# A planner that runs the chain between two stages first and holds long weight splits back for it

## The chip, the cores and the metric

The kernel runs on one core of one Trainium2 chip. The metric is the device time of one execution in microseconds (us), given as the median of the runs. PE is TensorE (matmuls), DVE is VectorE, ACT is ScalarE, POOL is GpSimd, SP is the engine that issues the transfers.

## The reference, cut to what matters

Two blocks of two layers each work on the same 256 tokens of width 1024, all in float32. Every layer is a mixer followed by a gated feed-forward network, and between any two of them stands the same small step: the product is scaled by a gate, added to the residual x, normed per token, and scaled and shifted per channel, which gives the input h of the next stage.

```python
h = modulate(rmsnorm(x, g_mix_pre[i]), sh_a, sc_a)
qkv = jnp.einsum('bsd,de->bse', h, w_qkv[i])
...
o = jnp.einsum('bse,ed->bsd', merge_heads(o), w_o[i])
x = x + gt_a[:, None, :] * rmsnorm(o, g_mix_post[i])
h = modulate(rmsnorm(x, g_ffn_pre[i]), sh_f, sc_f)
gate = jnp.einsum('bsd,df->bsf', h, w_ffn_gate[i])
up = jnp.einsum('bsd,df->bsf', h, w_ffn_up[i])
gate = causal_depthwise_conv(gate, w_conv[i], b_conv[i])
y = jnp.einsum('bsf,fd->bsd', jax.nn.silu(gate) * up, w_ffn_down[i])
x = x + gt_f[:, None, :] * rmsnorm(y, g_ffn_post[i])
```

The second block has the same frame without the norm behind the product, with a differential attention over tokens and context in its first layer and a short convolution in its second. In order there are eight stages: attention, feed-forward, attention, feed-forward, differential attention, feed-forward, short convolution, feed-forward.

## The kernel before, in words

**Arithmetic.** Each float32 operand of a large product is split into a high and a low part (`split`: a cast on ACT gives the high part, a subtraction on DVE the low part), and a product is three matmuls: high by high, high by low, low by high. A weight arrives from HBM as a chunk of 128 x 2048 (tile `w`, 1 MB). Each half of it is one long split: `wh` on ACT (128x1024) and `wl` on DVE (128x1024). The per-channel scales are made beside this by long DVE instructions over weight chunks (`w<-w,rows,vec`, 128x1024, called dots here). The small splits have names of their own: `oh`, `ol` and `doh`, `dol` for attention outputs, `yh`, `yl` for the feed-forward, `zhl` for the convolution, `h0h`, `h0l`, `h1h`, `h1l` for h.

**The boundary.** At the end of a stage, `last_products` adds the last terms to the accumulators `acc`: both halves of token tile 0 first, then token tile 1. `tail` then does, for token tile 0 and then 1: on DVE `u<-acc,rows` (gate) and `x` (residual) for two halves of 512; on ACT a sum of squares (`junk<-x`); on POOL a power (`ssr`); on DVE `u<-x,ssr` (the normed x); on PE eight transposes (`tps<-eye,u`); then on DVE and ACT scale and shift (`hf`) and the split into `h0h` and the rest. Where the product is normed too (the first block), a first sum of squares (`junk<-acc`) and power stand ahead of `x`. The next stage begins with `first_tiles`: two weight tiles over token tile 0 and then over token tile 1 (`fp`, 96 matmuls of 128x256), which are transposed afterwards (`fpt`). `rowps` are transposes that spread a gate over all rows. The two boundaries ahead of the second attention and of the differential attention have no `fp`; PE has other products there.

The boundaries with `fp` are named here A (first attention to feed-forward), C (second attention to feed-forward), E (differential attention to feed-forward), F (feed-forward to short convolution) and G (short convolution to feed-forward); B and D are the two without.

**The order.** The program is first recorded (`Rec.record`), each operation with a number `i` in program order and a modelled cost. `Rec.schedule` then plans all engines at once: at each model time, an engine that is free takes, of the operations whose inputs have arrived, the one with the lowest number (the heap `ready`); operations whose last input is already under way stand in `pending` with the time at which they arrive. Tiles come from a few lists of fixed size (`SLOTS`; PSUM has four banks of class `mm`, and a pair of score tiles `dz` takes two of them at once); weight splits (group `W`) and chunks (class `K8`) are handed out strictly in program order. `emit` writes the instructions in the planned order, so each engine works through a fixed queue on the chip. All profile rows carry the one line 573 of `emit`; a group is told by its tiles. In the model a cast `wh` costs 946 ns, a subtraction `wl` 1135 ns and the power 464 ns; a result of DVE reaches DVE's next instruction after another 127 ns.

Of the kernel before, what the change touches and what calls it, by code (L numbers as in the profile page):

```python
# [21 lines left out]
KT = D // P  # L22
# [237 lines left out]
class Op:  # L260
    __slots__ = ("i", "eng", "fn", "args", "kw", "deps", "outs", "tiles", "cost", "waits", "start", "end", "act", "dma")


class Rec:
# [4 lines left out]
    def __init__(self):  # L269
        self.ops, self.limit, self.count, self.after = [], 0, 0, None  # L270
        self.follow = {}
# [31 lines left out]
    def record(self, eng, fn, args, kw):  # L303
        op = Op()
        op.i, op.eng, op.fn, op.args, op.kw = len(self.ops), self.ENGINES[eng], fn, args, kw
        op.outs, op.deps, op.tiles, op.dma, op.act = [], {}, [], 0, 0
        outs = [kw[k] for k in ("out", "accum_out") if isinstance(kw.get(k), VAP)]
        ins = [v for k, v in kw.items() if k not in ("out", "accum_out") and isinstance(v, VAP)]
        pos = [a for a in args if isinstance(a, VAP)]
        if pos and "out" not in kw:  # L310
            outs.append(pos[0])
            pos = pos[1:]
        ins += pos
        if fn == "matmul" and not kw["start"]:
            v = outs[0]
            if any(w[0] & v.mask and w[1] < v.parts[1] and w[2] > v.parts[0] for w in v.t.writes):
                ins.append(v)
        for v in ins:
            self.access(op, v, False)
        for v in outs:  # L320
            self.access(op, v, True)
        if fn == "matmul" and kw["start"]:
            v = outs[0]
            for w in v.t.writes:
                if w[3] is not op and w[1] < v.parts[1] and w[2] > v.parts[0]:
                    op.deps.setdefault(w[3], 1)
        if self.after is not None:
            op.deps.setdefault(self.after, 1)
        for t in op.tiles:
            t.ops.append(op)  # L330
        op.cost = self.cost(op, outs, ins, args, kw)
        self.ops.append(op)
# [71 lines left out]
    def schedule(self, slots):  # L404
# [59 lines left out]
        while left:  # L464
# [14 lines left out]
            for e in engines:  # L479
                while pending[e] and pending[e][0][0] <= now:  # L480
# [3 lines left out]
                    else:  # L484
                        heapq.heappush(ready[e], (i, op))
            for e in engines:
# [6 lines left out]
                while ready[e]:  # L493
                    op = heapq.heappop(ready[e])[1]
                    if op in taken:
                        continue
                    lack = fits(op)
# [114 lines left out]
class Builder:  # L612
# [334 lines left out]
    def tail(self, acc, which, post, nxt):  # L947
        nc = self.nc
        g = self.gates[which]
        self.h = self.new_ht("h")  # L950
        for t in range(2):
# [4 lines left out]
            for a, b, c in zip(self.halves(u), y, self.halves(g)):  # L956
                nc.vector.tensor_tensor(out=a, in0=b, in1=c, op=ALU.mult)
            for a, b in zip(self.halves(u), self.halves(self.x[t])):
# [4 lines left out]
            self.put_ht(self.h, self.normed(self.x[t], u, self.xe[t]), t, *nxt)  # L963
        self.finish(*MODS)
# [201 lines left out]
    def attention1(self, i):  # L1166
# [13 lines left out]
        for it in range(KT + 2):  # L1180
# [17 lines left out]
            if 0 <= j < KT:  # L1198
# [3 lines left out]
                with nc.together():  # L1202
# [4 lines left out]
                    for hh in range(2):  # L1207
                        nc.tensor.matmul(
                            op[sl[hh], 128:256], lhsT=vs[1][:, cs[hh]], rhs=ats[hh][:, 256:384], start=False, stop=True
                        )  # L1210
                os_[j] = self.split(op[:, 0:256], S, "o")
            if it % 2 == 1 and it < KT:
# [15 lines left out]
    def ffn(self, b, i, nxt):  # L1228
# [5 lines left out]
        for f in range(NF + 1):  # L1234
# [14 lines left out]
            if f < NF:  # L1249
                s = self.sb.tile([P, S], F32, tag="s", name="s")  # L1250
# [13 lines left out]
                ys[f] = self.split(y, S, "y")  # L1264
                if f % 2 == 0:
# [116 lines left out]
    def diff_attention(self):  # L1382
# [67 lines left out]
        for it in range(U + VLAG + 3):  # L1450
# [3 lines left out]
            if it < U:  # L1454
# [23 lines left out]
                if m == 1:  # L1478
                    for hh in range(2):
# [8 lines left out]
                        es[it - 1 + hh] = p[0]  # L1488
            u = it - VLAG
# [21 lines left out]
            if 0 <= u < U and u % 4 >= 2:  # L1511
# [7 lines left out]
                if j % 2 == 0:  # L1519
                    w2[j], w2[j + 1] = wo.take()  # L1520
            j = it - WOFROM
# [22 lines left out]
    def short_conv(self):  # L1544
# [4 lines left out]
        for f in range(KT + 1):  # L1549
# [23 lines left out]
            if f % 2 == 1:  # L1573
# [4 lines left out]
                for k in range(2):  # L1578
                    z = self.sb.tile([P, S], F32, tag="z", name="z")
                    nc.vector.tensor_tensor(out=z, in0=zz[f - 1 + k], in1=ps[:, k * S : (k + 1) * S], op=ALU.mult)  # L1580
                    hl = self.sb.tile([P, 2 * S], F32R, name="zhl")
                    zz[f - 1 + k] = self.split_to((hl[:, 0:S], hl[:, S : 2 * S]), z)
                w2[f - 1], w2[f] = wd.take()
# [107 lines left out]
```

## Time and profile before

| | |
|---|---|
| median of 3 runs | 1337.94 us (1335.98 to 1338.98) |
| the profiled execution | 1337.94 us, span of its instructions 1335.9 us |
| PE matmul busy | 1301.9 us (97%) |
| DVE busy | 1082.9 us (81%) |
| ACT busy | 715.1 us (54%) |
| DMA, mean rate | 233 GB/s |

The time is the span and 2.0 us around it. Busy time counts an instruction from its start to its end; matmuls overlap, so PE can be busy and still start matmuls at half its pace.

### The profile page before, as it was taken

Reading aid. Unit: us, or ns where it says so; the run is one execution under the profiler, and the core shown is the slowest. Engines: PE = TensorE matmul, PEld = TensorE weight load, DVE = VectorE, ACT = ScalarE, POOL = GpSimd, SP = SyncE. Lnnn points to the kernel's source line nnn. Section 1 sums busy time; section 2 is a strip of 40 time slices with the busy share of each in tenths; the row PEclk is TensorE's granted clock in tenths of the full one; section 3 lists DMA queues with packets and bytes.
Section 4 is the critical chain, followed back from the end, with each engine's and each line's share of the span. In section 5 each row is a group of like instructions: output and inputs, shape, how many; then the busy total and the mean of one; then the engine's idle time right before and its main releaser. Section 6 shows DMA issues by size and latency. Waiting matters only on the chain.

```text
span 1335.9 us, 21951 instructions
## 1 busy us (share of the span) xinstructions
PE 1301.9 (97%) x8760; PEld 1172.1 (88%) x8760; DVE 1082.9 (81%) x1827; ACT 715.1 (54%) x1249; POOL 76.1 (6%) x102
## 2 busy tenths in 40 slices
PE   5999999999999999999999999899999999999998
PEld 4888799999898799999888777799999999999997
DVE  6899898998999699999799988876766998855542
ACT  3565755555666664556543667644444635644430
POOL 0000100000100000001033123100000000000000
PEclk9999999999999999999999999899999999999999
DMA  9866678887666357777454533577776587555520
GB/s 360 310 254 261 239 292 318 319 327 300 227 251 256 122 190 266 270 278 266 158 205 150 212 132 118 192 287 278 259 281 252 221 315 284 194 187 187 189 96 32
DMA packets 45319, 311.82 MB, mean 233 GB/s; under 512 B 5280, under 2 KB 5664, under 8 KB 8864
## 3 DMA queue, kind: packets, MB, share of 16 engines
q1 hardware_dynamic: 45216, 310.42, 62.4%
q8 instruction: 68, 1.11, 0.3%
q14 instruction: 35, 0.29, 0.1%
HBM read 309.35 MB, written 1.05 MB: 232 GB/s over the span
## 4 chain that ended last, share of the span: by engine, by line
PE 85%; DVE 6%; ACT 3%; issue 2%; DMA 1%; POOL 1%; SPq 0%; ACTq 0%; POOLq 0%; DVEq 0%
PE gu L573 34%; PE acc L573 28%; PE qkps L573 6%; PE fp L573 4%; PE cu L573 3%; DVE w L573 2%; PE bb L573 2%; PE qps L573 2%; PE z L573 2%; PE tps L573 1%; DMA w<-in_wst_dram 1%; PE op L573 1%; DVE wl L573 1%; PE kc L573 1%; PE atp L573 1%
## 5 line engine op out<-in xcount | busy, mean ns | idle before, releaser
L573 DVE TENSOR_TENSOR wl<-w,wh 128x1024 fp32r<-128x1024 f32 x392 | 470.5, 1220 | 71.5 <-ACT wh L573 47.9
L573 ACT CAST wh<-w 128x1024 fp32r<-128x1024 f32 x392 | 402.4, 1049 | 94.3 <-DMA w<-in_wst_dram 56.8
L573 DVE CUSTOM_DVE_ANT_0 w<-w,rows,vec 128x1024 f32<-128x1024 f32 x192 | 242.3, 1278 | 12.1 <-DMA w<-in_wst_dram 11.8
L573 PE MATMUL gu<-h1h,wh 128*128 128x256 f32 x640 | 181.3, 283 | 0.0
L573 PE MATMUL gu<-h1h,wl 128*128 128x256 f32 x640 | 181.2, 283 | 0.0
L573 PE MATMUL gu<-h0h,wl 128*128 128x256 f32 x640 | 181.1, 283 | 0.0
L573 PE MATMUL gu<-h1l,wh 128*128 128x256 f32 x640 | 181.1, 283 | 0.0
L573 PE MATMUL gu<-h0l,wh 128*128 128x256 f32 x640 | 181.1, 283 | 0.0
L573 PE MATMUL gu<-h0h,wh 128*128 128x256 f32 x640 | 180.9, 283 | 0.0
L573 PE MATMUL acc<-wh,yh 128*128 128x512 f32 x352 | 137.6, 392 | 0.0
L573 PE MATMUL acc<-wl,yh 128*128 128x512 f32 x352 | 137.4, 391 | 0.0
L573 PE MATMUL acc<-wh,yl 128*128 128x512 f32 x352 | 135.3, 389 | 0.0
L573 PEld LDWEIGHTS gu<-h0l,wh 128*128 128x128 f32 x640 | 122.6, 192 | 2.2
L573 PEld LDWEIGHTS gu<-h0h,wh 128*128 128x128 f32 x640 | 122.5, 192 | 2.3
L573 PEld LDWEIGHTS gu<-h1l,wh 128*128 128x128 f32 x640 | 122.8, 192 | 0.1
L573 PEld LDWEIGHTS gu<-h1h,wh 128*128 128x128 f32 x640 | 122.8, 192 | 0.1
L573 PEld LDWEIGHTS gu<-h1h,wl 128*128 128x128 f32 x640 | 122.8, 192 | 0.0
L573 PEld LDWEIGHTS gu<-h0h,wl 128*128 128x128 f32 x640 | 122.6, 192 | 0.0
L573 DVE TENSOR_TENSOR y<-s,gu 128x256 f32<-128x256 f32 x80 | 33.5, 418 | 74.6 <-ACT s L573 74.5
L573 ACT ACTIVATE s<-gu 128x256 f32<-128x256 f32 x40 | 15.4, 385 | 137.3 <-PE gu L573 137.3
L573 PEld LDWEIGHTS acc<-wh,yl 128*128 128x128 f32 x352 | 66.1, 188 | 14.3
L573 PEld LDWEIGHTS acc<-wh,yh 128*128 128x128 f32 x352 | 66.4, 189 | 12.2 <-ACT yh L573 0.2
(364 smaller groups left out, 2662.9 us busy)
## 6 DMA issues: line engine op xcount, KB each, us to landing
w<-in_wst_dram SPq DMA_DIRECT2D x284, 1024.0 KB, 4.9
w<-in_wst_dram SPq DMA_DIRECT2D x16, 512.0 KB, 11.4
x<-in_x_dram SPq DMA_DIRECT2D x2, 512.0 KB, 6.1
cx<-in_ctx_dram SPq DMA_DIRECT2D x2, 512.0 KB, 6.7
out_dram<-x SPq DMA_DIRECT2D x1, 512.0 KB, 2.6
out_dram<-x SPq DMA_DIRECT2D x2, 256.0 KB, 2.0
cst<-in_consts_dram SPq DMA_DIRECT2D x1, 264.0 KB, 5.5
smalls<-in_smalls_dram SPq DMA_DIRECT2D x1, 256.0 KB, 5.0
```

The costliest lines, as they stand in the source:

```text
L573: fn(*[real(a) for a in op.args], **{k: real(v) for k, v in op.kw.items()})
```

## The change

An operation recorded while `urgent` is set gets a key one million below its number, and the heap `ready` is ordered by the key. Set urgent are: all of `tail` (its PE transposes too), the split of the last attention output, the last two terms of a feed-forward network, everything of the differential attention that is recorded from turn 16 of its loop on (the last four pieces: transposes `dtp`, copies `dat`, products `dop`, norms, `of`, `doh`, `dol`, and one chunk of output weights with its splits) except its matmuls into `acc`, and the last terms of the short convolution. An operation that is not urgent and costs over 900 ns in the model (`wh`, `wl`, the dots) is put back when an urgent one stands in `pending` on its engine and arrives within 0.7 of that cost. In `tail`, each half's residual now follows its own gate, where both gates came first. The arithmetic is the same.

```diff
+        op.key = op.i - (10**6 if self.urgent else 0)
...
-                        heapq.heappush(ready[e], (i, op))
+                        heapq.heappush(ready[e], (op.key, op))
...
+                    if op.key >= 0 and op.cost > 900:
+                        t = min((p[0] for p in pending[e] if p[2].key < 0), default=math.inf)
+                        if t < now + 0.7 * op.cost:
+                            heapq.heappush(pending[e], (t, op.i, op))
+                            continue
...
+        nc.urgent = True
         for t in range(2):
...
-            for a, b, c in zip(self.halves(u), y, self.halves(g)):
-                nc.vector.tensor_tensor(out=a, in0=b, in1=c, op=ALU.mult)
-            for a, b in zip(self.halves(u), self.halves(self.x[t])):
+            for a, b, c, e in zip(self.halves(u), self.halves(self.x[t]), self.halves(g), y):
+                nc.vector.tensor_tensor(out=a, in0=e, in1=c, op=ALU.mult)
...
+        nc.urgent = False
...
+                nc.urgent = j == KT - 1
                 os_[j] = self.split(op[:, 0:256], S, "o")
...
+                nc.urgent = f >= NF - 2
...
+            nc.urgent = it >= U
...
+                    nc.urgent = f == KT - 1
```

## Rows read from the trace of the kernel before

**Rows 1.** The page: PE's busy time, and the chain that ended last by engine.
```profile
PE 1301.9 (97%) x8760; PEld 1172.1 (88%) x8760; DVE 1082.9 (81%) x1827; ACT 715.1 (54%) x1249; POOL 76.1 (6%) x102
PE 85%; DVE 6%; ACT 3%; issue 2%; DMA 1%; POOL 1%; SPq 0%; ACTq 0%; POOLq 0%; DVEq 0%
```

**Rows 2.** Busy time by stretch: the five boundaries A, C, E, F, G, from the last `acc` matmul of a stage to the last `fp` of the next. Columns: stretch, its length, busy time and (number of instructions) of PE, PEld, DVE, ACT and POOL, granted clock, DMA share, GB/s.
```profile
142.90:163.50 20.60, 17.32 (x119) 15.72 (x119) 19.50 (x36) 15.70 (x33) 3.24 (x4) 0.92 0.49 165
461.90:481.20 19.30, 18.48 (x150) 17.42 (x149) 17.85 (x34) 16.81 (x37) 1.10 (x2) 1.00 0.49 176
843.70:866.10 22.40, 18.19 (x123) 17.55 (x121) 18.08 (x35) 15.68 (x32) 2.02 (x2) 0.77 0.36 135
1042.20:1060.80 18.60, 17.55 (x141) 16.59 (x140) 18.16 (x37) 12.03 (x27) 1.66 (x1) 1.00 0.48 181
1138.90:1156.00 17.10, 16.44 (x131) 15.56 (x130) 14.39 (x30) 13.08 (x28) 1.17 (x1) 1.00 0.42 164
```

**Rows 3.** The chain that ended last, in order of time: start, length, what, how many. 48 matmuls of 128x256 and 16 transposes of 128x128 without a wait.
```profile
226.96 5.75 PE gu L573 x48
...
602.39 1.75 PE tps L573 x16
```

**Rows 4.** Who waited for whom on PE: us in total, times, longest.
```profile
PE tps L573 <- DVE u L573: 5.0, 2, 3.5
```

**Rows 5.** Busy time by stretch around boundaries A and E, columns as in Rows 2.
```profile
146.70:150.10 3.40, 3.35 (x15) 2.95 (x15) 3.40 (x9) 2.81 (x8) 0.00 (x0) 0.50 0.23 96
...
846.40:849.90 3.50, 1.95 (x8) 1.57 (x8) 3.50 (x7) 2.09 (x3) 1.98 (x2) 0.51 0.00 0
849.90:853.30 3.40, 2.67 (x13) 2.65 (x13) 2.92 (x10) 2.92 (x9) 0.00 (x0) 0.50 0.76 282
853.30:856.70 3.40, 3.40 (x18) 3.40 (x17) 2.50 (x8) 1.67 (x6) 0.00 (x0) 0.50 0.06 27
```

**Rows 6.** PE at boundary E in order of time: start, length, instruction, [idle before it and what ended it].
```profile
843.55 0.93 PE L573 MATMUL rowps<-eye,raw 128*128 128x128 f32 x7
847.95 1.97 PE L573 MATMUL tps<-eye,u 128*128 128x128 f32 x8 [3.47 <-DVE u L573]
850.65 0.58 PE L573 MATMUL fp<-wh,h0h 128*128 128x256 f32 x1 [0.73 <-ACT h0h L573]
```

**Rows 7.** ACT ahead of boundary E in order of time.
```profile
838.93 1.04 ACT L573 CAST wh<-w 128x1024 fp32r<-128x1024 f32 x1
839.87 0.40 ACT L573 CAST doh<-of 128x256 fp32r<-128x256 f32 x1
```

**Rows 8.** DVE ahead of boundary E in order of time.
```profile
840.00 1.23 DVE L573 TENSOR_TENSOR wl<-w,wh 128x1024 fp32r<-128x1024 f32 x1 [0.40 <-ACT wh L573]
841.14 0.42 DVE L573 TENSOR_TENSOR dol<-of,doh 128x256 fp32r<-128x256 f32 x1
841.48 1.22 DVE L573 TENSOR_TENSOR wl<-w,wh 128x1024 fp32r<-128x1024 f32 x1
842.62 1.28 DVE L573 TENSOR_TENSOR u<-acc,rows 128x512 f32<-128x512 f32 x2
```

**Rows 9.** PE at boundary F in order of time.
```profile
1042.11 1.03 PE L573 MATMUL tps<-eye,u 128*128 128x128 f32 x8
...
1044.28 0.39 PE L573 MATMUL fp<-wh,h0h 128*128 128x256 f32 x1 [0.27 <-ACT h0h L573]
```

**Rows 10.** DVE ahead of boundary F in order of time.
```profile
1034.14 0.69 DVE L573 TENSOR_TENSOR u<-acc,rows 128x512 f32<-128x512 f32 x1 [0.97 <-PE acc L573]
1034.75 1.28 DVE L573 CUSTOM_DVE_ANT_0 w<-w,rows,vec 128x1024 f32<-128x1024 f32 x1
...
1035.95 0.69 DVE L573 TENSOR_TENSOR x<-u,x 128x512 f32<-128x512 f32 x1
1036.55 2.36 DVE L573 TENSOR_TENSOR wl<-w,wh 128x1024 fp32r<-128x1024 f32 x2
1039.35 0.88 DVE L573 TENSOR_SCALAR u<-x,ssr 128x512 f32<-128x512 f32 x2 [0.44 <-POOL ssr L573]
```

**Rows 11.** DVE at boundary G in order of time.
```profile
1134.16 0.88 DVE L573 TENSOR_SCALAR u<-x,ssr 128x512 f32<-128x512 f32 x2 [0.79 <-POOL ssr L573]
```

**Rows 12.** PE at boundary G in order of time.
```profile
1138.78 1.03 PE L573 MATMUL tps<-eye,u 128*128 128x128 f32 x8
```

**Rows 13.** ACT at boundary C, token tile 1, in order of time.
```profile
468.36 1.09 ACT L573 CAST wh<-w 128x1024 fp32r<-128x1024 f32 x1
469.31 1.11 ACT L573 ACTIVATE junk<-x 128x1025 bf16<-128x1025 f32 x1
```

**Rows 14.** The power on POOL in order of time: at boundary F and at boundary G, both for token tile 0.
```profile
1037.96 1.36 POOL L573 TENSOR_TENSOR ssr<-ss,mhalf 128x1 f32<-128x1 f32 x1 [188.13 <-ACT junk L573]
...
1133.57 0.55 POOL L573 TENSOR_TENSOR ssr<-ss,mhalf 128x1 f32<-128x1 f32 x1 [83.77 <-ACT junk L573]
```

**Rows 15.** PE in the last turns of the differential attention in order of time: transposes of a piece, the last pair of scores `dz`, products of a piece.
```profile
820.95 0.60 PE L573 MATMUL dtp<-eye,p 128*128 128x128 f32 x4
821.48 0.98 PE L573 MATMUL dz<-kT11h,qT1h 64*128 64x512 f32 x2
...
823.37 0.83 PE L573 MATMUL dop<-dv,dat 128*128 128x128 f32 x6
```

**Rows 16.** DVE in the same turns: the norm that empties that product's bank.
```profile
829.36 0.35 DVE L573 TENSOR_SCALAR on<-dop,rstd 128x128 f32<-128x128 f32 x1
```

More of the change, by code (lines that the diff above doesn't have):

```diff
@@ L260 @@
 class Op:
-    __slots__ = ("i", "eng", "fn", "args", "kw", "deps", "outs", "tiles", "cost", "waits", "start", "end", "act", "dma")
+    __slots__ = ("i", "eng", "fn", "args", "kw", "deps", "outs", "tiles", "cost", "waits", "start", "end", "act", "dma", "key")
 class Rec:
@@ L270, in __init__ @@
         self.ops, self.limit, self.count, self.after = [], 0, 0, None
+        self.urgent = False
         self.follow = {}
@@ L1210, in attention1 @@
                         )
+                nc.urgent = j == KT - 1
                 os_[j] = self.split(op[:, 0:256], S, "o")
+                nc.urgent = False
             if it % 2 == 1 and it < KT:
@@ L1264, in ffn @@
                 ys[f] = self.split(y, S, "y")
+                nc.urgent = False
                 if f % 2 == 0:
@@ L1520, in diff_attention @@
                     w2[j], w2[j + 1] = wo.take()
+            nc.urgent = False
             j = it - WOFROM
@@ L1582, in short_conv @@
                     zz[f - 1 + k] = self.split_to((hl[:, 0:S], hl[:, S : 2 * S]), z)
+                nc.urgent = False
                 w2[f - 1], w2[f] = wd.take()
```

## The prediction

> **What bounds the kernel now.** I read the page first: PE is busy 97% of the span and the chain that ended last runs through PE for 85% [rows 1]. What a change of order can win is therefore only time in which PE starts matmuls late, and busy time hides that, because a matmul counts until its end. So I went on to the chain in order of time for the pace: 48 matmuls of 128x256 take 5.75 us, 120 ns each, and 16 transposes 1.75 us, 109 ns each [rows 3]. The change works at the boundaries, so the third view is the busy time of the five with `fp` [rows 2]. Each holds 96 `fp` (11.52 us); the other PE instructions, 23 to 54, are priced at 0.109 to 0.12. What is left of the stretch is lost:
>
> A: 20.6 - 11.5 - 23 x 0.11 = 6.6 us. C: 19.3 - 11.5 - 54 x 0.11 = 1.9. E: 22.4 - 11.5 - 27 x 0.11 = 7.9. F: 18.6 - 11.5 - 45 x 0.115 = 1.9. G: 17.1 - 11.5 - 35 x 0.11 = 1.7. Together 20.0 us, 1.5% of the time: the ceiling of what the boundaries can give. B and D, where PE has other products, show no wait of PE for the tail: among PE's waits the normed x (`u`) stands with two places in all, 5.0 us, the longest 3.5 [rows 4], and these are A (1.5) and E.
>
> **The change part by part.**
>
> *What it costs in instructions:* nothing is added or removed, and the sums of durations stay. The new order of gate and residual in `tail` swaps instructions of one engine with equal inputs; I put it at nothing.
>
> *E, the chain ahead of the tail.* PE stands idle 3.47 us until the first transposes and 0.73 us from the transposes to `fp` [rows 6]. What came late is the last split of the attention output. `doh` starts at 839.87 as the long cast before it ends, which ran from 838.93 [rows 7]: 0.94 us. `dol` starts at 841.14 as `wl` ends, though `doh` had ended at 840.27 [rows 7, 8]: 0.87 us. Both pieces are urgent now and the long ones aren't, so `dol` ends about 1.8 us earlier. Then `u` starts at 842.62 as a third long one ends [rows 8]; how long it had been ready no row tells, so it counts zero to 1.1 us more, and I take zero. PE has `acc` matmuls until 843.55 in any case, so an earlier `dol` lets token tile 0 finish first and token tile 1 cover its tail: the idle 3.47 us shrink by 1.8. The pieces before it (`dtp`, `dop` and their copies) gain on `acc` too; bounds from nothing to the 1.7 us left of that idle time, taken as nothing.
>
> *E, the clock.* The granted clock is 0.51, 0.50 and 0.50 in the three stretches from 846.4 to 856.7, 10.3 us at the lower of its two levels; PE had had no matmul since 844.48 when it fell [rows 5, 6]. Its price from the rows: 8 transposes in 1.97 us against 0.87 at full pace (1.1 us); 13 instructions in 2.67 us and 18 in 3.40 us, 0.205 and 0.189 each, against 0.12 (1.1 and 1.2 us) [rows 5, 6]; together 3.4 us. With 1.8 us less idle time the clock may stay up (3.4 us won), or fall as before (nothing). Boundary A is the nearest row: there PE idled 1.5 us for its transposes [rows 4] and the clock was at 0.5 for one stretch of 3.4 us, 15 instructions in 3.35 us, 0.22 each, which costs 15 x 0.10 = 1.5 us [rows 5]. I take E to become like A: 3.4 - 1.5 = 1.9 us won. E in all: 1.8 + 1.9 = 3.7 us.
>
> *F, token tile 0.* After the gate of the second half DVE runs a dot from 1034.75, and the residual `x` follows at 1035.95 [rows 10]. `x` is then pending and urgent and due within 0.13 us by the planner's lag, so the dot is held: 1.2 us less. The normed x is finished at 1040.23 [rows 10] but its transposes run at 1042.11 [rows 9], because PE takes the lower number, and the `acc` matmuls of token tile 1 have it. As urgent ones they go ahead by 1.9 + 1.2 = 3.1 us, and the way from transposes to `fp`, 2.17 us of which 8 transposes and 8 `rowps` fill 1.74 [rows 9], is covered by `acc` matmuls that would have run before. Of the 1.9 us lost at F I take 1.3; the rest lies with token tile 1, whose chain is unchanged but for its start. Bounds: nothing to 1.9.
>
> *G* is alike without the dot: normed x finished at 1135.04 [rows 11], transposes at 1138.78 [rows 12], so 3.7 us to go ahead by. Of 1.7 us I take 1.2; bounds nothing to 1.7.
>
> *C.* For token tile 1 the sum of squares starts at 469.31 as a long cast ends that began at 468.36 [rows 13]: up to 0.95 us won where the planner sees `x` coming, which it does, as `x` was placed before. With the transposes of token tile 0 in front of `acc`, I take 1.1 of 1.9 us; bounds nothing to 1.9.
>
> *A.* No row shows a long instruction in front of a step of its tail. I take 0.5 us; bounds nothing and the 1.5 us that PE idles there.
>
> *What is held and moved back.* Each held split idles its engine for at most 0.7 of its modelled cost, 0.66 us on ACT and 0.79 us on DVE. That is free while the next stage's splits are ahead of PE, and it costs its length once they aren't; F is the place to look, as DVE is busy 18.16 of 18.6 us there [rows 2]. One hold on the path at each of five boundaries would cost 4.0 us, none costs nothing; the DVE had 4.3 us free in E and 2.7 in G [rows 2], so I take nothing. Transfers: the tail issues none. In the differential attention one urgent chunk and its two splits are recorded; chunks and split tiles are handed out in program order, so SP's queue keeps its order. On PE the urgent transposes now stand in front of `acc` matmuls, which wait if the normed x is late (a rival, below).
>
> *One rule of the skill.* The power on POOL takes 0.55 us at G and 1.36 at F, where two `wl` run back to back from 1036.55 to 1038.91 around its start at 1037.96 [rows 10, 14]; it ends 0.41 us after the second. The Trainium skill, page "SBUF — State Buffer", section "Who interferes with whom", says that VectorE and GpSimd share a port pair as an exclusive lock, and that an instruction of VectorE with two SBUF inputs blocks a GpSimd instruction that reads SBUF for its whole length; this trace agrees (1.36 against 0.55 us). By that rule a hold that kept `wl` out of the power's way would be worth 0.8 us per boundary; my sum has nothing for it, since the planner sees the normed x coming only when it has placed the power, and the second `wl` starts before that.
>
> **Sum.** 0.5 + 1.1 + 3.7 + 1.3 + 1.2 = 7.8 us. The profiled execution took 1337.94 us (span 1335.9 and 2.0 around it) and is also the median of the runs. 1337.9 - 7.8 = 1330.1, -0.6%. About 0.2% (2.7 us) is what a measurement can tell from no change.
>
> **The rivals.**
>
> *The last scores lose their banks (slower).* Pieces 12 and 13 are urgent and ready before the last pair `dz`, which needs two of four PSUM banks at once. Now the pair runs at 821.48 right behind one piece's transposes [rows 15]. A piece's product keeps its bank from 823.37 to the norm at 829.36 [rows 15, 16], so two pieces in front could delay the pair by 6.3 us. Pieces 14 and 15 hang on it and the last terms on them; PE runs dry, +6.3, the clock falls for longer, +2, and E's gain is gone: 1337.9 - 4.1 + 8.3 = 1342.1. It is slower by over 0.2% once the delay passes some 5 us. Against it: the piece's chain would also be finished sooner under the urgent key, and banks with it.
>
> *The holds don't bite.* The planner sees an urgent operation only when its last input is under way, and the tail already had lower numbers than the next stage's splits. Then only PE's order changes, and E stays as it is: 1337.9 less 2 = 1336. For it: the long casts in front of `doh` and `junk` started within 0.1 us of being passed over [rows 7, 13], so a model a little off lets them through again.
>
> *The power comes free of the splits.* Were the planner to see the normed x early enough, about 0.8 us more at A (two tiles), E and F: 1330.1 - 3.2 = 1326.9. It needs a hold 1.3 us ahead, which the 0.79 us don't reach.
>
> *Transposes in front, normed x late.* The model gives the power 464 ns and the chip up to 1.36 us [rows 14]; PE then stops at the transposes with `acc` matmuls queued behind. 0.9 us at C, F, B and D would cost 3.6 us and leave 1333.7. Against it: B and D already have transposes in front of other products, and no wait for `u` beyond A and E is listed [rows 4].
>
> **How the numbers follow.** Forecast (1326.5 to 1333.5 by its bounds) 0.55; holds don't bite 0.14; late normed x 0.11; power free 0.10; lost banks 0.10. The time is that of the likeliest, 1330.1. Below 1324.5 lie the power free together with an E whose clock stays up, some 0.06; above 1337.5 the lost banks and a small part of the holds that don't bite, some 0.13; so the range is 1324.5 to 1337.5. Faster by over 0.2% (below 1335.2): 0.55 + 0.10 + most of late normed x (0.08) + little of the second (0.03) = 0.76. Slower (above 1340.6): 0.08. Same: 0.16.
>
> **What would show it.** Right: at E `doh` directly behind `of`, `dol` behind that, less than 2 us idle before `tps`, and a stretch at 0.5 no longer than A's; at F, G and C `tps` of token tile 0 with `acc` matmuls behind them, and `x` right behind its `u` at F. Wrong: waits of PE for `u` at C, F or G, or of `gu` and `cu` for `wl`; `dz` later than the products of pieces 12 and 13; the 0.5 stretch at E as long as now, or new ones elsewhere.

## The result, and the profile after

The changed kernel takes 1357.41 us (1356.41 to 1358.7) against 1338.16 of the kernel before beside it: ratio 1.0145, interval 1.0129 to 1.016. It is slower by 1.4%, where I had forecast 0.6% faster and given "slower" 8 in 100.

The page of the kernel after: PE's busy time, and the chain that ended last by engine, as in [rows 1]. PE is as busy as before; of the chain, DVE holds 13% instead of 6%.

```profile
PE 1306.0 (96%) x8760; PEld 1172.6 (87%) x8760; DVE 1083.7 (80%) x1827; ACT 717.2 (53%) x1249; POOL 74.3 (5%) x102
PE 76%; DVE 13%; DMA 3%; ACT 3%; issue 2%; POOL 2%; SPq 0%; POOLq 0%; ACTq 0%; DVEq 0%
```

Busy time is no guide to 19 us, so I cut the span at starts of PE instructions that both kernels have: the last `op` product of each plain attention, the last `fp` of each boundary, the first `kc` (the first product of the differential attention). The stretches add up to the spans, 1335.9 and 1355.1 us. Each is read from one profiled execution.

| stretch | before | after | difference | forecast |
|---|---|---|---|---|
| start, first attention | 134.27 | 134.31 | 0.0 | 0 |
| boundary A | 28.88 | 30.81 | +1.9 | -0.5 |
| feed-forward 1, B, second attention | 282.83 | 283.09 | +0.3 | 0 |
| boundary C | 34.93 | 34.37 | -0.6 | -1.1 |
| feed-forward 2, D | 177.79 | 185.26 | +7.5 | 0 |
| differential attention, E | 207.05 | 220.06 | +13.0 | -3.7 |
| feed-forward 3, F | 194.75 | 192.49 | -2.3 | -1.3 |
| short convolution, G | 95.19 | 94.42 | -0.8 | -1.2 |
| feed-forward 4 | 180.18 | 180.27 | +0.1 | 0 |

The instruction at a cut is the same in both kernels, but another order puts other matmuls ahead of it. In the kernel after, eight transposes `rowps<-eye,cact` and four `gu`, products of the feed-forward (1.4 us at the pace of [rows 3]), have moved from C's stretch into that of feed-forward 2, and four `fpt` and four `cu`, products of the convolution (0.9 us), out of F's into later ones.

The busy time of the five boundaries A, C, E, F, G in the kernel after, cut and laid out as in [rows 2]:

```profile
143.00:165.40 22.40, 17.34 (x114) 16.42 (x115) 18.30 (x36) 14.55 (x31) 1.88 (x4) 0.85 0.44 171
466.20:482.90 16.70, 15.89 (x130) 15.33 (x129) 14.89 (x26) 14.01 (x30) 1.10 (x2) 1.00 0.37 129
868.30:888.20 19.90, 16.51 (x114) 16.08 (x115) 14.65 (x32) 12.53 (x27) 2.02 (x2) 0.83 0.16 54
1065.50:1080.70 15.20, 14.72 (x124) 14.51 (x123) 14.19 (x27) 7.41 (x16) 1.42 (x1) 1.00 0.39 132
1160.70:1175.10 14.40, 14.40 (x121) 14.25 (x120) 13.06 (x23) 11.21 (x20) 0.55 (x1) 1.00 0.37 133
```

By the prediction's own arithmetic (96 `fp` for 11.5 us, the rest at 0.11, at F 0.115), which counts what stands in each boundary, they lose 8.9, 1.5, 6.4, 0.5 and 0.1 us, where it had 6.6, 1.9, 7.9, 1.9 and 1.7. At F and G almost nothing is left to win. The loss lies ahead of E, in feed-forward 2, and at A.

**Ahead of E.** PE in the last turns of the differential attention of the kernel after, in order of time (idle before in brackets); the row of before that answers is the last pair `dz` in [rows 15]. The pair ahead of that one, in the kernel before:

```profile
816.80 0.50 PE L573 MATMUL dz<-kT01h,qT0h 64*128 64x512 f32 x2
```

The kernel after:

```profile
827.31 0.50 PE L580 MATMUL dz<-kT01h,qT0h 64*128 64x512 f32 x2
...
835.21 0.27 PE L580 MATMUL dop<-eye,on 128*128 128x128 f32 x1
...
838.14 0.33 PE L580 MATMUL dop<-eye,on 128*128 128x128 f32 x1
...
843.49 0.55 PE L580 MATMUL dop<-eye,on 128*128 128x128 f32 x3 [2.27 <-DVE on L580]
...
848.06 0.50 PE L580 MATMUL dz<-kT11h,qT1h 64*128 64x512 f32 x2
...
854.54 0.63 PE L580 MATMUL dtp<-eye,p 128*128 128x128 f32 x4 [0.94 <-DVE drs L580]
...
859.35 0.33 PE L580 MATMUL dop<-eye,on 128*128 128x128 f32 x1
...
861.61 0.48 PE L580 MATMUL dop<-eye,on 128*128 128x128 f32 x1
...
870.95 1.66 PE L580 MATMUL tps<-eye,u 128*128 128x128 f32 x8 [2.66 <-DVE u L580]
```

The last pair starts 20.75 us after the pair ahead of it (before: 4.68), behind the products of pieces 10 to 13. Pieces 14 and 15 (`dtp` from 854.54) hang on it.

What holds the banks so long are tiles that stand half filled. The transposes `dop<-eye,on` of two pieces share one bank (9 with 11, 12 with 14, 13 with 15), which is read only when both halves are in; which row belongs to which piece follows from the planner's order. With their small keys pieces 12 and 13 open their banks at 835.21 and 838.14. The other halves are those of pieces 14 and 15, at 859.35 and 861.61, and these need the last pair itself. So two of the four banks stay taken beyond the pair. A third was half filled by piece 9 until piece 11, which has no small key and fell behind 12 and 13, came with the transposes at 843.49.

The granted clock falls three times. Busy time of three stretches of the kernel after, columns as in [rows 5]:

```profile
843.90:847.40 3.50, 3.04 (x13) 2.72 (x12) 1.43 (x3) 2.92 (x7) 0.00 (x0) 0.52 1.00 375
861.00:864.50 3.50, 3.50 (x10) 2.38 (x10) 1.11 (x3) 1.83 (x3) 0.17 (x1) 0.51 0.92 325
871.20:878.10 6.90, 6.17 (x30) 5.73 (x29) 6.36 (x18) 4.71 (x14) 1.07 (x1) 0.51 0.00 0
```

That is 13.9 us at the lower level against 10.3 [rows 5], two of the three falls ahead of the boundary.

**Feed-forward 2.** Its background begins with sixteen transposes that spread two condition vectors over all rows (`rowps<-eye,cact`, eight for each) and their four copies (`rows`), which the long dots after them read. In the kernel before, the last of the transposes on PE and the first dot on DVE:

```profile
471.21 0.81 PE L573 MATMUL rowps<-eye,cact 128*128 128x128 f32 x6
...
477.99 1.28 DVE L573 CUSTOM_DVE_ANT_0 djunk<-w,rows,vec 128x1024 bf16<-128x1024 f32 x1
```

In the kernel after, first the transposes on PE, in order of time, the eight of the second vector 38 us behind those of the first:

```profile
472.64 1.03 PE L580 MATMUL rowps<-eye,cact 128*128 128x128 f32 x8
...
510.87 1.03 PE L580 MATMUL rowps<-eye,cact 128*128 128x128 f32 x8
```

The last copies on ACT and the first dot on DVE:

```profile
511.58 1.06 ACT L580 COPY rows<-rowps 128x512 f32<-128x512 f32 x2
...
512.88 1.28 DVE L580 CUSTOM_DVE_ANT_0 djunk<-w,rows,vec 128x1024 bf16<-128x1024 f32 x1
```

And who waited for whom on PE from 480 to 660 us (in total, times, longest), as in [rows 4]:

```profile
PE acc L580 <- ACT yh L580: 3.3, 3, 1.4
```

Now the dots begin 35 us later and come close together, between the steps of `y`, and PE waits for `yh` three times; with the waits of `gu` there it is 4.5 us. Before, no wait of PE is listed there at all.

### The profile page after: what moved, and what is told of

Its sections match the earlier page's. It is cut to its first block, busy times and chain, and to the rows that moved or that the text cites. A ratio compares the mean times of both kernels' runs of the same rounds, so it can differ in the third digit from the quotient of the medians.

```text
span 1355.1 us, 21939 instructions
## 1 busy us (share of the span) xinstructions
PE 1306.0 (96%) x8760; PEld 1172.6 (87%) x8760; DVE 1083.7 (80%) x1827; ACT 717.2 (53%) x1249; POOL 74.3 (5%) x102
## 4 chain that ended last, share of the span: by engine, by line
PE 76%; DVE 13%; DMA 3%; ACT 3%; issue 2%; POOL 2%; SPq 0%; POOLq 0%; ACTq 0%; DVEq 0%
PE gu L580 31%; PE acc L580 23%; PE qkps L580 5%; PE fp L580 4%; DVE w L580 3%; DMA w<-in_wst_dram 3%; PE cu L580 3%; DVE wl L580 2%; PE bb L580 2%; POOL rstd L580 2%; PE qps L580 1%; PE z L580 1%; DVE djunk L580 1%; PE tps L580 1%; DVE dmx L580 1%
## 5 line engine op out<-in xcount | busy, mean ns | idle before, releaser
L580 PEld LDWEIGHTS acc<-wh,yl 128*128 128x128 f32 x352 | 66.0, 188 | 13.8
```

Source lines behind the costliest of these rows:

```text
L580: fn(*[real(a) for a in op.args], **{k: real(v) for k, v in op.kw.items()})
```

## The experiments

In the expectations, "lost PE time" is the time from one matmul's start to the next less the usual time of that kind in the kernel before, summed over a stage. The results, by the stretches of the table above, each ratio against the kernel before run beside it (1337.2 to 1338.4 us; F stands for feed-forward 3 and F, G for the short convolution and G). The first stretch, which is not in the table, lies between 133.4 and 136.4 us, though little of it is changed in any of them:

| kernel | time, us | ratio to before (interval) | A | C | ff 2, D | diff., E | F | G |
|---|---|---|---|---|---|---|---|---|
| before | 1338 | | 28.9 | 34.9 | 177.8 | 207.1 | 194.8 | 95.2 |
| after | 1357.4 | 1.0145 (1.0129, 1.0160) | 30.8 | 34.4 | 185.3 | 220.1 | 192.5 | 94.4 |
| e1 | 1342.7 | 1.0031 (1.0021, 1.0042) | 30.5 | 34.4 | 184.6 | 208.0 | 192.5 | 94.4 |
| e2 | 1350.4 | 1.0073 (1.0053, 1.0092) | 28.9 | 35.0 | 178.2 | 217.1 | 194.8 | 95.2 |
| e3 | 1353.2 | 1.0104 (1.0089, 1.0119) | 30.1 | 34.8 | 178.1 | 219.2 | 195.0 | 96.3 |
| e4 | 1334.8 | 0.9963 (0.9948, 0.9977) | 29.9 | 34.2 | 180.2 | 200.8 | 193.7 | 95.6 |
| e5 | 1347.5 | 1.0074 (1.0057, 1.0091) | 30.8 | 34.4 | 186.4 | 212.9 | 191.7 | 94.4 |
| e6 | 1342.7 | 1.0046 (1.0030, 1.0063) | 30.8 | 34.4 | 185.0 | 206.2 | 192.5 | 94.4 |
| e7 | 1341.5 | 1.0033 (1.0019, 1.0048) | 30.6 | 34.8 | 177.9 | 210.3 | 192.5 | 94.4 |
| e8 | 1356.5 | 1.0138 (1.0118, 1.0158) | 30.6 | 34.4 | 186.6 | 219.8 | 192.5 | 94.4 |
| e9 | 1332.0 | 0.9952 (0.9937, 0.9966) | 30.6 | 34.8 | 177.9 | 200.9 | 192.8 | 94.0 |
| e10 | 1338.7 | 1.0006 (0.9993, 1.0018) | 32.0 | 34.8 | 178.0 | 207.1 | 192.8 | 94.7 |
| e11 | 1358.8 | 1.0155 (1.0136, 1.0173) | 32.0 | 34.4 | 185.0 | 222.1 | 192.8 | 94.7 |
| e12 | 1334.5 | 0.9973 (0.9963, 0.9982) | 28.9 | 34.2 | 180.2 | 202.7 | 193.8 | 95.6 |
| e13 | 1331.0 | 0.9949 (0.9936, 0.9963) | 28.9 | 33.7 | 177.9 | 202.3 | 192.8 | 94.0 |
| e14 | 1331.9 | 0.9957 (0.9944, 0.9969) | 30.2 | 34.8 | 177.9 | 202.8 | 192.9 | 94.7 |
| e15 | 1332.7 | 0.9964 (0.9952, 0.9975) | 30.6 | 32.0 | 177.9 | 202.7 | 192.9 | 94.7 |

### Parts of the change: e1 to e4

e1 takes away the flag in the differential attention, e2 keeps that flag alone, e3 takes away the hold, e4 keeps the hold alone.

```diff
-            nc.urgent = it >= U                        # e1
+            nc.urgent = False
-                nc.urgent = f >= NF - 2                # e2: this and the other three flags
+                nc.urgent = False
-                    if op.key >= 0 and op.cost > 900:  # e3
+                    if False:
-                        heapq.heappush(ready[e], (op.key, op))  # e4
+                        heapq.heappush(ready[e], (op.i, op))
```

> The change without the urgent flag of the differential attention's last pieces; the rest as it is. Theory 1 (the last score pair waits for PSUM banks behind pieces 12 and 13): the pair of scores comes back to its place behind piece 12's transposes, boundary E loses what it lost before or less, and some 12 us of the 19 come back: 1345. Theory 2 (the held splits delay the stream of weights everywhere): little comes back, 1353 to 1357. Theory 3 (urgent steps overtake the small steps they wait for, as the scale of boundary A): as theory 2, 1353 or more.

> Of the urgent flags only that of the differential attention's last pieces is left; keys and holds as in the change, so holds act only there. Theory 1: most of the loss stays with this flag alone, 1338 + 12 = 1350. Theories 2 and 3: near the kernel before, 1337 to 1340.

> Keys and flags as in the change, but no operation is held back. Theory 2: the splits run as early as before, the waits of the second feed-forward network and of the start of the differential attention go, 1347 or less. Theories 1 and 3: the keys alone make the loss, 1354 to 1358.

> The ready list is ordered by number again, as before the change; flags and holds stay, and the gate and residual of a half stand together. Theory 2: the loss of the second feed-forward network and of the differential attention's start is here, 1344 to 1348. Theories 1 and 3: nothing is overtaken, so no bank is taken early, 1335 to 1339.

The times of e1 and e2 are near those of the first theory; e3 (1353.2) lies just below the range of its theories and e4 (1334.8) just below its own. The flag on the pieces costs the stretch with E 12.1 us in the whole change (220.1 to 208.0) and 10.0 when nothing else has a flag (207.1 before, 217.1 in e2). The hold is not what hurts there: without it the stretch is as long (219.2), and alone it is the only part that wins. In e4 eleven matmuls that otherwise stand behind the cut ahead of the differential attention stand ahead of it, so its two stretches are read together: 381.0 us against 384.9, 3.9 won, about the gain that I had forecast for E. Boundary E in e4, from the last `acc` to the last `fp`, columns as in [rows 2], shows the clock at its upper level throughout:

```profile
847.20:864.20 17.00, 15.78 (x122) 14.44 (x121) 16.73 (x33) 15.09 (x32) 0.65 (x1) 1.00 0.45 156
```

In e2 it is the pair before the last that is held up most. Its PE rows in order of time, the three last pairs:

```profile
813.74 0.50 PE L580 MATMUL dz<-kT11h,qT1h 64*128 64x512 f32 x2
...
828.39 0.51 PE L580 MATMUL dz<-kT01h,qT0h 64*128 64x512 f32 x2
...
835.36 0.50 PE L580 MATMUL dz<-kT11h,qT1h 64*128 64x512 f32 x2
```

Feed-forward 2 loses its 7 us only where the other small keys and the hold are both there (after and e1, not e2 or e3; in e4 the 2.4 us are mostly the matmuls that moved). The gain of F and G needs both too: their two stretches together win 3.0 us in after and 0.7 with the hold alone (e4), and lose 1.3 without the hold (e3).

### Who takes the banks: e5 and e6

e5 puts the last pair itself in front, e6 sets the flag only for pieces 14 and 15, which read that pair's weights and so can't overtake it.

```diff
+            nc.urgent, nc.after = it >= U - 1, prev if it == U - 1 else None   # e5, ahead of the pair
...
-            nc.urgent = it >= U                                                # e6
+            nc.urgent = it >= U + 2
```

> The whole change, with one addition: the last score pair of the differential attention (turn 15: its dz products, maxima, exponentials and the weighting of p) gets the same small key as pieces 12 to 15, and may start once the exponentials of the pair before it are issued. Theory of the banks: in the changed kernel pieces 12 and 13 take the PSUM banks that the last pair needs, its dz starts at 848.06 us, 20.7 us after the pair before it (before: some 4 us), and the differential attention with boundary E loses 44.8 us of PE time where the kernel before loses 32.1. With the pair ahead of the pieces its dz starts within 8 us of the pair before it, that stage falls to 32.1 us or below, and the time to 1357.4 - 12.7 = 1344.7 us (1339 to 1347). Rival: the pieces' numbers hurt by themselves (they push the splits and the dots of the diff stage aside, whatever the pair does): the pair starts early and the time stays above 1352.

> The whole change, but in the differential attention only pieces 14 and 15 get the small keys (the flag is set from turn U + 2 instead of U), so that nothing which can run before the last score pair is in front of it. Theory of the banks: pieces 14 and 15 read the last pair's own weights and cannot overtake it, so the last dz starts some 4 to 8 us after the pair before it, the stage loses 32 us or less, and the time is 1344.7 (1339 to 1347), as with the pair put in front. Rival (the pieces' numbers hurt by themselves): half of the harm stays, 1350 or more.

With e6 the last pair starts 5.88 us after the pair ahead of it and the stretch with E is 13.8 us shorter than in after, as the theory of the banks has it. PE in e6, its two last pairs:

```profile
826.81 0.50 PE L580 MATMUL dz<-kT01h,qT0h 64*128 64x512 f32 x2
...
832.69 0.50 PE L580 MATMUL dz<-kT11h,qT1h 64*128 64x512 f32 x2
```

The planner's own record agrees: in the change it passes the last pair over 15 times for want of a PSUM bank and places it at 788.5 us of its model time; without the flag (e1) 5 times, and it is placed at 776.6. By the same record the banks of pieces 12 with 14 and 13 with 15 stay taken for 22 to 23 us each in the change, 18 to 23 in e2 and e3, 18 in e7, but 2 to 5 in the kernel before and in e1, e6 and e9; the stretch with E is longest where they are held longest. No run takes away these half-filled tiles alone.

e5 missed: its pair starts 6.88 us after the one before, yet the stretch gains 7.2 us of the 13.8 and the time, 1347.5, lies just above the range. Pieces 12 and 13 in front cost something beyond the pair's start. In e5 PE waits 5.3 us between 805 and 880 where e6 waits 2.3, and the clock falls for 6.8 us there, which it does not in e6. One half-filled bank is left in e5: that of pieces 9 and 11 is held for 21 us of the planner's time, against 2 in e6. Whether that is the whole cause stays open.

### The spreading of the condition vectors: e7

```diff
+                self.nc.urgent = True
                 self.cb[k] = self.on_all_rows(self.cact[:, k * 8 : k * 8 + 8])
+                self.nc.urgent = False
```

> The whole change, with one addition: the four transposes and copies that spread the condition vectors over all rows (rows <- rowps, at the start of the second feed-forward's background) get the small key. In the changed kernel they ran at 511.6 and 512.1 us instead of 465 to 472, the background's dots began 46 us after the stage's first product instead of 14, and feed-forward 2 lost 6.6 us of PE time instead of 0.55. Theory (the big copies lose their 4 KB slots to the splits and drag the stage's weight stream with them): the dots begin within 20 us, the stage loses under 1 us, the time falls by 5.5 to 6 us, to 1351.5 (1350.5 to 1353). Rival (the stage loses because the held splits themselves come late at its start, whatever the copies do): the stage still loses 4 us or more, 1356 or more.

The last of the transposes on PE and the first dot on DVE in e7:

```profile
443.46 1.15 PE L580 MATMUL rowps<-eye,cact 128*128 128x128 f32 x9
...
488.67 1.28 DVE L580 CUSTOM_DVE_ANT_0 djunk<-w,rows,vec 128x1024 bf16<-128x1024 f32 x1
```

Feed-forward 2 is whole again (177.9), PE waits for nothing in it, and the stretch with E gains 9.8 us on top. So the time falls by 15.9 us and not by 6. Of the 9.8 us, 5.3 come also where the pair is cured already (e6 to e9): the background's lateness had gone on into the differential attention. The rest goes with the pair, which is delayed less in e7: the last two pairs start 11.17 and 6.23 us behind the ones ahead of them, 17.4 together, where it was 25.4 in the kernel after. The expectation named the wrong tile: by the planner's record the last eight transposes are refused twice, at 441.3 and 443.5 us, for want of a PSUM bank and not of a 4 KB slot. By that record boundary C is the gap in which PE ran them before, with nothing of a lower number to do; at the two refusals transposes of the tail, the first `fpt` and an earlier tile of the spreading itself fill the four banks; past the gap, the products of the feed-forward have lower numbers, and the eight are planned for 475 and run at 510.87. What the hold adds to this I did not take apart further.

### Both cures together: e9

```diff
-            nc.urgent = it >= U
+            nc.urgent = it >= U + 2
...
+                self.nc.urgent = True
                 self.cb[k] = self.on_all_rows(self.cact[:, k * 8 : k * 8 + 8])
+                self.nc.urgent = False
```

> The whole change, with both cures of a PSUM bank lost to a step with a small key: the spreading of the condition vectors over all rows in front (as in e7), and small keys in the differential attention for pieces 14 and 15 alone (as in e6). Theory (the whole loss of the change is work that must come soon and has no small key, overtaken at two places, and the two losses add): e7's time less what its end of the differential attention still loses against e6, 14.8 + 3.7 - 8.5 - 2.8 = 7.2 us of PE time: 1341.5 - 7.2 = 1334.3 (1332 to 1337), 0.2% faster than before, with F and G still at 0.9 and 0.3 us. Rival (the two losses are one and the same lateness carried on, and don't add): 1338 or more.

1332.0 us, the lower end of what was expected (1332 to 1337). Apart, the two cures give 14.7 (e6) and 15.9 us (e7), together 25.4, so the two losses add but for some 5 us. The change with these two edits is 0.5% faster than the kernel before. E in e9, columns as in [rows 2], has no stretch at the lower clock:

```profile
847.30:864.20 16.90, 14.74 (x123) 14.19 (x122) 15.62 (x32) 13.32 (x31) 1.10 (x2) 1.00 0.25 86
```

### Boundary A: e8 and e10 to e15

First boundary A in the kernel after. The scale `msc_f` has no small key, though the first `hf`, which has, reads it; it runs behind all of token tile 1's residual, and PE waits 3.20 us. The scale in the kernel before, then DVE and PE in the kernel after:

```profile
139.04 0.15 DVE L573 SCALAR_TENSOR_TENSOR msc_f<-raw,vec 128x8 f32<-128x8 f32 x1
```

```profile
145.51 1.41 DVE L580 SCALAR_TENSOR_TENSOR x<-u,ssr,x 128x512 f32<-128x512 f32 x2
146.84 0.16 DVE L580 SCALAR_TENSOR_TENSOR msc_f<-raw,vec 128x8 f32<-128x8 f32 x1
147.11 1.37 DVE L580 TENSOR_SCALAR hf<-tps,msc_f,msh_f 128x128 f32<-128x128 f32 x4
...
148.34 0.58 PE L580 MATMUL fp<-wh,h0h 128*128 128x256 f32 x1 [3.20 <-ACT h0h L580]
```

e8 gives the scale a small key:

```diff
+                self.nc.urgent = kind == "sc_f" and b == 0
                 for key in (kind, "c" + kind)[: 1 + ctx_too]:
                     self.scale_of(b, i, kind, 0, 8, key)
+                self.nc.urgent = False
```

> The whole change, with one addition: the small DVE step that makes the scale vector of the feed-forward's h (msc_f <- raw, vec) gets the small key in both attention stages of the first block. In the changed kernel boundary A lost 9.15 us of PE time instead of 6.79: the scale ran at 146.84 us instead of 139.04, because it had no small key though the steps with small keys wait for it, and the hf after it at 147.11 instead of 145.31. Theory of the overtaken small step: the scale runs before 144, the 3.2 us gap of PE at A falls to about 1.4, boundary A loses 6.8 us or less, and the time falls by 2.4 us, to 1355.0 (1354 to 1356.3). Rival (the dot ahead of the scale, which is long and held, is what is late): A stays above 8.5 and the time at 1357.

DVE and PE at A in e8: the scale runs at 141.30 and the first `fp` at 144.41, and the second one then waits for a held split.

```profile
141.30 0.17 DVE L580 SCALAR_TENSOR_TENSOR msc_f<-raw,vec 128x8 f32<-128x8 f32 x1
...
148.00 1.21 DVE L580 TENSOR_TENSOR wl<-w,wh 128x1024 fp32r<-128x1024 f32 x1
```

```profile
144.41 0.38 PE L580 MATMUL fp<-wh,h0h 128*128 128x256 f32 x1 [0.79 <-ACT h0h L580]
149.26 0.58 PE L580 MATMUL fp<-wl,h0h 128*128 128x256 f32 x1 [4.47 <-DVE wl L580]
```

So the scale's place was cured and the gain did not come: A is almost as long as without the cure (30.6 against 30.8), because the next wait stood behind it. e10 (on e9), e11 (on the change) and e12 (on e4) give the splits of the first two weight tiles small keys, e10 and e11 the scale as well; in e12, where the order goes by number, the key only keeps them from being held:

```diff
+        nc.urgent = True
         ws = [self.w.take() for f in range(n)]
+        nc.urgent = False
```

> As e9, and at boundary A both steps that e8's trace showed late: the scale of h gets the small key (as in e8), and so do the splits of the two weight tiles that the first fp products read, so that they are no longer held back for the chain. In e8 the scale came 5.5 us earlier and PE's first fp product 3.9 us earlier, but its second then waited 4.47 us for the held split wl, and boundary A lost 8.90 us as before. Theory (a held split that the next product reads is itself on the path): boundary A loses 4 to 5.5 us, and the time is e9's less 3.5 to 5, some 1330.3 (1328 to 1332.5), faster than the kernel before by 0.4 to 0.7%. Rival (a 1.2 us split let into the chain costs it as much as it saves): A stays above 8 us and the time at e9's.

> The whole change, with the two cures of boundary A alone (scale and splits of the first two weight tiles with small keys). Theory (held split on the path): boundary A falls from 9.15 us to 4 to 5.5, nothing else changes but C's and E's first splits, and the time is 1357.4 - 4 = 1353.4 (1352 to 1355). Rival (splits let into the chain cost as much): 1356 or more.

> The hold alone (the ready order is that of the kernel before, as in e4), but the splits of the first two weight tiles of a stage are never held. In e4 boundary A lost 8.28 us against 6.79 before, 1.88 of it in one wait of PE for the held wl at 151.9. Theory: that wait goes, the rest of e4's gain stays, 1334.75 - 1.9 = 1332.9 (1331.5 to 1334). Rival (the split then stands ahead of the chain's own steps, as before): A stays at 6.8 or more and C or E give back part of e4's gain, 1334.5 or more.

All three missed. DVE and PE at A in e10: splits stand ahead of the normed x twice, the dot that the scale reads is put off with it, and PE waits 5.24 us for `u`.

```profile
146.00 2.35 DVE L580 TENSOR_TENSOR wl<-w,wh 128x1024 fp32r<-128x1024 f32 x2
148.80 1.00 DVE L580 TENSOR_SCALAR u<-x,ssr 128x512 f32<-128x512 f32 x2 [0.44 <-POOL ssr L580]
...
151.03 0.17 DVE L580 SCALAR_TENSOR_TENSOR msc_f<-raw,vec 128x8 f32<-128x8 f32 x1
```

```profile
149.55 1.94 PE L580 MATMUL tps<-eye,u 128*128 128x128 f32 x8 [5.24 <-DVE u L580]
```

e10 gives back all that e9 won (A 1.4 us, the stretch with E 6.2). e12 is as fast as e4 within the intervals: A gains 1.0 and the stretch with E loses 1.9, as its rival had it. The clock at E goes with these two numbers: it is at its lower level for 6.8 us in e10 and 3.4 in e12, and not at all in e9 and e4.

e13, e14 and e15 are built on e9: no small keys at A; the scale in front and the first splits at their old place but never held; those splits unheld alone.

```diff
-        nc.urgent = True                     # e13, in tail; alike for the last attention output
+        nc.urgent = self.late                # False in the first attention alone
...
-                    if op.key >= 0 and op.cost > 900:                                  # e14, e15
+                    if op.key >= 0 and op.cost > 900 and op.i not in self.nohold:
```

> As e9, but without small keys at boundary A: the last pair of the first attention and the chain from its last product to the feed-forward's h keep their places in the program's order there, so the hold finds nothing to hold for. Theory (at A the small keys do the harm: they let the chain overtake the scale that it needs itself, and they make the hold keep back the split that PE reads next): boundary A loses 6.8 us as before the change, and the time is e9's less 2.1, 1329.9 (1328.5 to 1331.5). Rival (A's loss comes from the order of the stage ahead of it and not from A's own keys): A stays above 8.5 and the time at 1332.

> As e9, with the scale in front (small key) and the splits of the first two weight tiles of each feed-forward and of the short convolution at their old place in the order but never held back for the chain. Theory (the scale and the hold are the two causes, one behind the other): in the 2.7 us in which DVE waits for the power of the first half it makes one of these splits, no wait of PE for a held wl is left at A, boundary A loses 5 to 6.5 us, and the time is e9's less 2.5 to 4, 1328 to 1329.5. Rival (any split that is let in delays the chain by its 1.2 us, as in e10): A loses 8 or more, 1331 or more.

> As e14, without the scale in front. Theory (the scale is the first cause): it still runs after the chain's second half, PE's first fp product waits some 3 us for hf as in the changed kernel, and A loses 8 to 9 us, 1331.5 to 1332.5. Rival (the hold is the only cause): A falls to 6.8 or less, 1330 or less.

Without small keys A has its old length (28.9), so it is these that cost A its 1.9 us; but the second attention, planned in another order, took the gain back in waits of some 0.6 us each, and e13 (1331.0) can't be told from e9. In e15 A stays as long as in e9 (its C looks shorter because twelve matmuls into `acc` stand ahead of the cut). In e14 A gets only 0.4 us shorter than in e9 and the wait moves on to another `wl` (1.62 us at 150.66). Yet PE's waits at A add up to 3.5 us in e14 and 5.9 in e9. Most of these 2.4 us went to the clock, by the estimate below: in e14 it is at its lower level for 10.2 us of A, where e9 has 3.4. Busy time of that stretch in e14, columns as in [rows 2]:

```profile
146.30:156.50 10.20, 8.56 (x39) 8.27 (x39) 8.31 (x16) 5.69 (x11) 2.33 (x3) 0.50 0.39 125
```

At 0.12 us each the 39 matmuls would fill 4.7 us instead of 8.6, so the lower level costs 3.9 us by this estimate, where the prediction priced 3.4 us of it at 1.5. Why the clock fell for longer with shorter waits, no run shows. DVE is busy for 18.30 of A's 22.4 us in after and for 19.50 of 20.6 before [rows 2]; in e8, e10, e11 and e15, whatever was put in front there, something that PE needed next came late.

## Why the prediction was wrong, step by step

- *The lost banks of the last scores* is the step that failed first. I had the place and the direction, gave it a chance of 0.10 and priced the delay at 6.3 us from one product's hold on its bank [rows 15, 16]. The pair starts 20.75 us behind the one before it instead of 4.68: a delay of 16 us. The hold that counts was not in the sum: the next tile of pieces 12 and 13, half filled, which keeps its bank until pieces 14 and 15 have come, and these wait for the pair. "The piece's chain would also be finished sooner" was right (the norms `on` of pieces 12 and 13 run 5.8 and 9.5 us behind the pair ahead of the last, before 12.6 and 16.0), but not that its banks would be: it opened these tiles so early. e6 shows the loss, 13.8 us.
- *What is held and moved back*, taken as nothing, is the second step that failed. I asked what each hold keeps back and answered for the splits alone ("free while the next stage's splits are ahead of PE"). I did not list the other steps that somebody waits for soon and that lived in the gaps: the spreading of the condition vectors (7.5 us in feed-forward 2, and 15.9 in all with what it carries on, e7) and, at A, the scale and the first split that `fp` reads.
- *A:* +1.9 us instead of -0.5. "No row shows a long instruction in front of a step of its tail" holds for the rows listed and is beside the point: a short one that the tail reads fell behind it, and the splits that PE reads next were held. The small keys at A cost it the 1.9 us (e13); how these share between the two stays open, as neither cure brought them back (e8, e14).
- *E, chain and clock:* right in its mechanism, hidden by the pair. In the kernel after, the last `doh` and `dol` do follow at once (862.63 and 863.06), but 23 us late. Where no bank is lost the stretch with E wins 6.2 us (e9) against the forecast 3.7: the clock, which I took to fall once as at A, does not fall at all. Where it does fall once, for 3.4 us (e13 to e15), 4.3 to 4.8 us are won.
- *F and G* came as forecast: transposes of token tile 0 at 1061.20 and 1156.21, as the normed x is made (before, 1.9 and 3.7 us behind it [rows 9 to 12]). By the stretches 2.3 and 0.8 us are won against 1.3 and 1.2; by the lost time of the boundaries themselves, which leaves out the matmuls that moved, 1.4 and 1.6. *C* won 0.4 of 1.1 by the same count, and in e9 0.1 by its stretch.
- Of the other rivals, *the holds don't bite* falls with e4 and e3. *Normed x late* did not occur: PE's waits for `u` in the kernel after are 4.1 us at three places, A (1.1) and E (2.7) two of them. *The power free of splits* did not come either; see below.
- *The bounds* of the parts add up to a time between 1324.0 and 1336.1, not to the 1326.5 to 1333.5 written beside the chances.

With the two overtaken steps put right the time comes out near the forecast: e9 is at 1332.0, inside its range and 1.9 us from its time. That close a hit is partly luck, as in e9 A loses 1.7 us instead of winning 0.5, C wins 0.1 instead of 1.1, and E wins 2.5 us more than forecast.

## What to carry to other kernels

When some steps of a planned kernel are put in front, list what is left without a mark and is needed soon: what the marked steps read, what shares a pool of banks with them, and what lived in the gaps that they fill. A step that needs two banks at once loses to every one that needs one. Ask of each marked step not only which bank it takes but what must come before that bank is free again: a tile that a marked step opens, and that can close only behind an unmarked one, keeps its bank for all the time between them. Mark only what can't overtake its own suppliers (here the last two pieces and not the last four), and try the hold apart from the order: the hold alone won, the order as it was made lost. The order with its two cures and without the hold was not run.

## What the runs showed of the hardware

The power on POOL, DVE's dots beside it at F, and the same power at G, in the kernel after:

```profile
1058.84 1.28 DVE L580 CUSTOM_DVE_ANT_0 w<-w,rows,vec 128x1024 f32<-128x1024 f32 x1
...
1059.05 1.49 POOL L580 TENSOR_TENSOR ssr<-ss,mhalf 128x1 f32<-128x1 f32 x1 [186.21 <-ACT junk L580]
...
1154.33 0.55 POOL L580 TENSOR_TENSOR ssr<-ss,mhalf 128x1 f32<-128x1 f32 x1 [83.76 <-ACT junk L580]
```

At F it is a dot now that the power sits out, 1.49 us, ending 0.42 us after it, as it sat out the splits before [rows 10, 14]. The Trainium skill, page "SBUF — State Buffer", section "Who interferes with whom", gives such a lock for a VectorE instruction with two SBUF inputs; the trace agrees, as it did before. The hold did not keep the dots away.

PE's idle time at E alone did not decide the clock there. In e9 PE waits 0.91 us for `u` and 1.25 for `h0h`, and the clock stays at its upper level; in e13, with the same two waits to 0.01 us, the profiled execution (1332.9 us; the six lie between 1328.3 and 1333.0) had it at the lower one for 3.4 us:

```profile
850.10:853.50 3.40, 3.30 (x15) 3.30 (x16) 1.99 (x7) 2.66 (x9) 0.48 (x1) 0.50 0.00 0
```

Between those two the stretch with E differs by 1.4 us, and e13 to e15, each with one such fall there, are 1.4 to 1.9 us above e9. My step "E becomes like A" priced the clock from one row of A at 1.5 us for a fall, which fits; but a gain or loss of that size hangs on more than the wait in front of it, and what more, these runs do not show.
